# Low parts of projection weights made by an accumulating DMA instead of a VectorE subtraction

## The chip, the cores and the metric

The kernel runs on one core of a Trainium2 chip. The time is the device time of one execution, in microseconds; the kernel before has a median of 1444.12 us over three runs (1443.51 to 1444.13).

A core has five engines, each with its own queue of instructions, worked off in order: TensorE (PE) for matmuls, VectorE (DVE) and ScalarE (ACT) for elementwise work, GpSimd (POOL), and SyncE (SP), whose queue issues the DMAs. They wait for each other by semaphores. In this kernel a DMA is issued by SP, and after the change also by GpSimd.

## The reference

One layer on 1024 tokens of width 1024, all in float32. A mixer has two branches that start from one projection of `x`: forgetting attention with 8 heads of 64, and a gated linear recurrence (HGRN) with 4 heads of 128. Each branch is projected back to 1024 columns, weighted with a sigmoid gate, the two are added and projected once more. After a residual and a layer norm follows a SwiGLU network with 2816 hidden columns, another residual and another layer norm.

```
proj = x @ w_in
q_a, k_a, v_a, f_a, q_b, f_b, i_b, g_b, gate_a, gate_b = jnp.split(proj, IN_SPLITS, axis=-1)
...
merged = jax.nn.sigmoid(gate_a) * (y_a @ w_pa) + jax.nn.sigmoid(gate_b) * (y_b @ w_pb)
mix = merged @ w_o
```

## The kernel before

Every large product is made with operands split in two. The high part is the number rounded to the matmul's reduced format (`float32r`), the low part is what is left, and a product is three matmuls that add up in PSUM: high by high, high by low, low by high (`mm3`, line 449). The high part comes from ScalarE and the low part from VectorE (`split`, line 420):

```
def split(hi, lo, src):
    act.copy(hi, src)
    dve.tensor_sub(lo, src, f(hi))
```

Many of the products also go through a Strassen-Winograd scheme, which saves matmuls and costs VectorE additions. The change does not touch those. It touches the weights that are used plainly, through `weights` (line 437). Such a weight block of 128 rows by 1024 columns is loaded by SP into a raw tile (`wr0` or `wr1`, one buffer each) and split in two halves of 128 x 512, each with its own high tile and low tile (`wh0`, `wl0`, `wh1`, `wl1`, two buffers each). `weights` is called for:

- the q and k projections of head pairs 1 to 3 (`wq`, `wk`: 6 blocks), between the attention of one pair and the next;
- the three projections of each of the four HGRN heads (`wb`: 12 blocks);
- four gate blocks (`wg`) and four half gate blocks (`we`), which run beside attention and HGRN;
- the branch projections (`wp`: 8 blocks).

That is 34 blocks and 68 splits. The matmuls of a block stand in `project` (line 460), except those of `we`, which are in `gate_part` (line 1047). `project` runs over the eight chunks of 128 rows (four for `wp`) and makes the three matmuls of each chunk, for each half of 512 tokens.

The order of the work is not that of the source. Every call is recorded by `Plan`, which knows a cost for each operation (`cost`, line 131), a latency between engines (`LAT`, `OWN`) and the buffers, and places the calls one after another where they can start earliest (`schedule`, line 170). It does so for up to 20 rounds with ranks that come from the latest possible starts of the round before (`latest`, line 294), keeps the order with the earliest planned end, and writes each engine's calls in that order (`issue`, line 352). `early` lets the calls of a weight rank before their place in the source. The order of each engine is fixed when the program is built; on the chip a late operand makes the engine wait.

## Time and profile before

| | |
|---|---|
| median of three runs | 1444.12 us |
| span of the profiled execution, first to last instruction | 1441.5 us (its whole time is not given apart) |
| granted TensorE clock | 0.998 |
| PE busy | 1430.0 us, 99% |
| DVE busy | 1112.8 us, 77% |
| ACT busy | 668.6 us, 46% |
| POOL busy | 87.2 us, 6% |
| DMA on SP's queue | 180.11 MB, 37.9% of the 16 engines' span |

All instructions of the main part have line 363 in the profile, because they are issued from one helper. They are told apart by their tiles: `wb_h` and `wb_l` are high and low parts of an HGRN weight, `bps` the PSUM tile of its product, `gps`, `ge` and `pps` those of `wg`, `we` and `wp`, `gs` the gates made by the Strassen scheme, `fa`, `fb`, `fc` and `p` the products of the SwiGLU network.

### The profile page before, as it was taken

Reading aid. Unit: us, or ns where it says so; the run is one execution under the profiler, and the core shown is the slowest. Engines: PE = TensorE matmul, PEld = TensorE weight load, DVE = VectorE, ACT = ScalarE, POOL = GpSimd, SP = SyncE. Lnnn points to the kernel's source line nnn. Section 1 sums busy time; section 2 is a strip of 40 time slices with the busy share of each in tenths; the row PEclk is TensorE's granted clock in tenths of the full one; section 3 lists DMA queues with packets and bytes.
Section 4 is the critical chain, followed back from the end, with each engine's and each line's share of the span. In section 5 each row is a group of like instructions: output and inputs, shape, how many; then the busy total and the mean of one; then the engine's idle time right before and its main releaser. Section 6 shows DMA issues by size and latency. Waiting matters only on the chain.

```text
span 1441.5 us, 18901 instructions
## 1 busy us (share of the span) xinstructions
PE 1430.0 (99%) x6782; PEld 1188.2 (82%) x6782; DVE 1112.8 (77%) x1952; ACT 668.6 (46%) x1167; POOL 87.2 (6%) x100
## 2 busy tenths in 40 slices
PE   9999999999999999999999999999999999999997
PEld 7788888888888888788888888888888888888886
DVE  8998778567998999845857997666677776798596
ACT  5547768667767663344511443323333334434330
POOL 0002213120100110000000000000000000000011
PEclk9999999999999999999999999999999999999999
DMA  7022212211111455858500233233333326977632
GB/s 270 32 89 67 95 60 74 63 60 51 38 59 46 153 170 164 255 181 290 176 0 2 102 95 124 96 110 110 110 110 110 97 92 201 346 276 235 209 129 85
DMA packets 74029, 181.30 MB, mean 126 GB/s; under 512 B 8384, under 2 KB 9792, under 8 KB 73936
## 3 DMA queue, kind: packets, MB, share of 16 engines
q1 hardware_dynamic: 73936, 180.11, 37.9%
q8 instruction: 53, 0.87, 0.3%
q14 instruction: 40, 0.33, 0.1%
HBM read 139.90 MB, written 40.17 MB: 125 GB/s over the span
## 4 chain that ended last, share of the span: by engine, by line
PE 97%; DVE 2%; DMA 1%; issue 0%; ACT 0%; SPq 0%; DVEq 0%; ACTq 0%
PE p L363 14%; PE fb L363 12%; PE bps L363 9%; PE fc L363 8%; PE fa L363 8%; PE o L363 6%; PE pps L363 6%; PE gs L363 5%; PE vx L363 4%; PE gps L363 3%; PE s L363 2%; PE pv L363 2%; PE qps L363 2%; PE kps L363 2%; PE vy L363 2%; PE pt L363 2%
## 5 line engine op out<-in xcount | busy, mean ns | idle before, releaser
L363 PE MATMUL p<-dp 128*128 128x512 f32 (+1 forms) x957 | 210.1, 382 | 0.0
L363 PEld LDWEIGHTS p<-dp 128*128 128x128 f32 x957 | 175.1, 188 | 34.8
L363 PE MATMUL fc<-xs,Tp 128*128 128x512 f32 x528 | 127.3, 389 | 0.6 <-ACT Tp L363 0.6
L363 PE MATMUL fb<-xs,Tp 128*128 128x512 f32 x528 | 127.2, 389 | 0.0
L363 PEld LDWEIGHTS fc<-xs,Tp 128*128 128x128 f32 x528 | 99.1, 188 | 21.6 <-ACT Tp L363 1.0
L363 PEld LDWEIGHTS fb<-xs,Tp 128*128 128x128 f32 x528 | 99.1, 188 | 20.5
L363 PE MATMUL fa<-x,Tp 128*128 128x512 f32 x480 | 115.6, 389 | 0.0
L363 ACT CAST Tp<-t 128x512 fp32r<-128x512 f32 x88 | 54.2, 619 | 118.8 <-PE fc L363 64.8
L363 DVE TENSOR_TENSOR Tp<-t,Tp 128x512 fp32r<-128x512 f32 x88 | 60.6, 690 | 60.5 <-ACT Tp L363 59.9
L363 PEld LDWEIGHTS fa<-x,Tp 128*128 128x128 f32 x480 | 90.1, 188 | 18.7
L363 PE MATMUL bps<-xh,wb_h 128*128 128x512 f32 x192 | 76.2, 397 | 0.0
L363 PE MATMUL bps<-xl,wb_h 128*128 128x512 f32 x192 | 76.0, 396 | 0.0
L363 PE MATMUL bps<-xh,wb_l 128*128 128x512 f32 x192 | 75.5, 396 | 0.0
L363 POOL TENSOR_TENSOR norm<-norm,mhalf 128x1 f32<-128x1 f32 x16 | 17.2, 1075 | 886.3 <-DVE norm L363 886.3
L363 ACT CAST dp<-dap 128x1024 fp32r<-128x1024 f32 (+1 forms) x42 | 41.0, 979 | 57.8 <-PE p L363 35.7
L363 POOL TENSOR_SCALAR p<-p,soft 128x384 f32<-128x384 f32 (+4 forms) x64 | 51.9, 817 | 261.0 <-DVE soft L363 235.2
L363 DVE TENSOR_TENSOR tl<-pt,th 128x512 fp32r<-128x512 f32 (+1 forms) x96 | 52.2, 554 | 19.7 <-ACT th L363 15.5
L363 ACT CAST th<-pt 128x512 fp32r<-128x512 f32 (+1 forms) x96 | 45.5, 479 | 34.9 <-PE pt L363 30.8
L363 DVE TENSOR_TENSOR dp<-dap,dp 128x1024 fp32r<-128x1024 f32 (+1 forms) x42 | 47.4, 1132 | 15.9 <-ACT dp L363 15.7
L363 PE MATMUL fb<-x,Tp 128*128 128x512 f32 x240 | 57.7, 389 | 0.0
L363 PE MATMUL pt<-ident,p 128*128 128x128 f32 x288 | 53.8, 273 | 0.0
L363 ACT CAST Tp<-wg_r 128x512 fp32r<-128x512 f32 x40 | 24.9, 623 | 62.1 <-PE fb L363 30.2
(565 smaller groups left out, 3476.6 us busy)
## 6 DMA issues: line engine op xcount, KB each, us to landing
dbp<-in_w_fo SPq DMA_DIRECT2D x45, 512.0 KB, 5.3
dap<-a_d SPq DMA_DIRECT2D x35, 512.0 KB, 4.3
wg_r<-in_w_ff SPq DMA_DIRECT2D x22, 512.0 KB, 4.0
wu_r<-in_w_ff SPq DMA_DIRECT2D x22, 512.0 KB, 3.6
a_d<-ar SPq DMA_DIRECT2D x42, 256.0 KB, 2.7
a_d<-as SPq DMA_DIRECT2D x33, 256.0 KB, 3.4
wg_r<-in_w_g SPq DMA_DIRECT2D x16, 512.0 KB, 4.4
sg<-gate_d SPq DMA_DIRECT2D x32, 256.0 KB, 3.4
```

What stands on the lines that cost most here:

```text
L363: getattr(q.engine, method)(*args, **kw)
```

## The change

The high part stays a copy by ScalarE. The low part is no longer a subtraction on VectorE. ScalarE writes the negated high part into the low tile, and GpSimd issues a DMA that adds the same 128 x 512 part of the raw weight from HBM onto it. In `project`, all matmuls with the high part of the weight come first and those with the low part last, so that a block's low part is first read 16 matmuls after its high part (8 for `wp`). `gate_part` keeps its order.

The planner learns of the new DMA: it costs GpSimd's queue 1000 ns, its data counts as landed 2300 ns plus bytes/200 ns later, and a fourth one waits until the first of three has landed. The space for descriptors of GpSimd's DMAs grows from 256 to 512. Since the planner weighs all calls together, the order changes on all engines, in stages with no such weight too.

```diff
+RING = 3
...
+    SOFT, LANDS = 1000.0, 2300.0
...
-        if method == "copy_predicated":
+        if method == "copy_predicated" or "accum_op" in kw:
             ins.append(outs[0])
...
+        self.lands.append(self.LANDS + o_bytes(outs[0]) / 200.0 if q.name == "POOL" and method == "dma_start" else 0.0)
...
         if eng == "POOL":
+            if method == "dma_start":
+                return self.SOFT
...
+        ring = [0.0] * RING
...
+                    if self.lands[i]:
+                        t = max(t, ring[-RING])
...
-                fin = t + d
-                free[q] = fin
+                free[q] = t + d
+                fin = t + d + self.lands[i]
+                if self.lands[i]:
+                    ring.append(fin)
...
-        lat = self.OWN[q] if uq == q else self.LAT[q]
+        lat = self.lands[i] + (self.OWN[q] if uq == q else self.LAT[q])
...
-            split(hi, lo, raw[:, i * n:(i + 1) * n])
+            part = slice(i * n, (i + 1) * n)
+            act.copy(hi, raw[:, part])
+            act.activation(lo, f(hi), AF.Copy, scale=-1.0)
+            pool.dma_start(lo, src[:, part], accum_op=ALU.add)
...
         for c in range(kcs):
             rh, rl = (src or X)(c)
-            mm3(o, *w[c], rh[:, hs(hf)], rl[:, hs(hf)], c == 0, c == kcs - 1)
+            mm(o, w[c][0], rh[:, hs(hf)], start=c == 0, stop=False)
+            mm(o, w[c][0], rl[:, hs(hf)], start=False, stop=False)
+        for c in range(kcs):
+            mm(o, w[c][1], (src or X)(c)[0][:, hs(hf)], start=False, stop=c == kcs - 1)
...
-    nc = bacc.Bacc("TRN2", target_bir_lowering=False, num_devices=1, dynamic_dma_scratch_size=256)
+    nc = bacc.Bacc("TRN2", target_bir_lowering=False, num_devices=1, dynamic_dma_scratch_size=512)
```

More of the change, by code (lines that the diff above doesn't have):

```diff
@@ L54, in __getattr__, with o_bytes @@
         return lambda *args, **kw: self.plan.add(self, method, args, kw)
+def o_bytes(ap):
+    return ap.partition_size() * ap.free_size() * 4
 class Plan:
@@ L69, in __init__ @@
         self.early = 0
+        self.lands = []
         self.loose = set()
@@ L303, in latest @@
             for m in by.get(old, ()):
-                users[m].append((i, self.LAT[calls[m][0].name] + 60))
+                users[m].append((i, self.lands[m] + self.LAT[calls[m][0].name] + 60))
         preds = [[] for _ in calls]
```

## The prediction

> **What bounds the kernel now.** I read the engine totals first, then TensorE's own waits, then stretches of the span, and last the chain.

> ```profile
> span 1441.5 us, 18901 instructions
> PE 1430.0 (99%) x6782; PEld 1188.2 (82%) x6782; DVE 1112.8 (77%) x1952; ACT 668.6 (46%) x1167; POOL 87.2 (6%) x100
> ```

> TensorE (PE) is busy for all but 11.5 us. Every other engine has room as a mean, but a mean says little, so the waits come next (engine, line, what was waited for: total us, times, longest).

> ```profile
> PE vy L363 <- DVE mhalf L363: 1.2, 1, 1.2
> PE gs L363 <- DVE gu L363: 1.2, 2, 0.8
> PE fc L363 <- ACT Tp L363: 0.6, 1, 0.6
> ```

> Those three are all the waits the trace finds for PE: 3.0 us, one of them at the very start. None is in a stage that uses `weights` and `project`. The next view has busy time by stretch: attention with the q/k projections and plain gates, the recurrence (HGRN) with its projections, the half gates, and the branch projections.

> ```profile
> core 0: us, PE busy (x) PEld busy (x) DVE busy (x) ACT busy (x) POOL busy (x), PEclk, DMA share, GB/s
> 100.00:324.00 224.00, 223.98 (x1205) 188.31 (x1204) 165.28 (x497) 159.36 (x340) 51.88 (x64) 1.00 0.24 77
> 324.00:480.00 156.00, 156.00 (x839) 133.89 (x838) 133.53 (x218) 109.87 (x185) 10.32 (x12) 1.00 0.18 55
> 480.00:520.00 40.00, 40.00 (x228) 34.67 (x228) 36.98 (x55) 26.28 (x53) 3.54 (x2) 1.00 0.57 190
> 600.00:710.00 110.00, 109.64 (x484) 90.55 (x483) 70.33 (x106) 51.78 (x80) 0.00 (x0) 1.00 0.65 219
> ```

> PE is full in all four although VectorE reaches 86% (133.53 of 156) and 92% (36.98 of 40). A full PE can still hide short delays, since a matmul is on record for 0.39 us and the next starts earlier.

> ```profile
> 327.76 21.84 PE bps L363 x96
> 308.83 0.38 PE L363 MATMUL pt<-ident,p 128*128 128x128 f32 x2
> 308.97 0.31 PE L363 MATMUL pv<-tl,vhl 128*128 128x128 f32 x1
> 309.16 0.49 PE L363 MATMUL bps<-xh,wb_h 128*128 128x512 f32 x1
> 309.49 0.39 PE L363 MATMUL bps<-xl,wb_h 128*128 128x512 f32 x1
> 309.72 0.39 PE L363 MATMUL bps<-xh,wb_l 128*128 128x512 f32 x1
> ```

> From the chain, 96 projection matmuls take 21.84 us, 0.2275 each; a 128-wide one takes 0.07 (two from 308.83 to 308.97). From 309.16 to 309.49 is 0.33, so about 0.1 us of delay can hide between two matmuls. The change leaves number and widths of the matmuls as they are. So the floor stays, and only delays can be won or lost.

> **The change, part by part.**

> *VectorE.* 68 subtractions for low parts go.

> ```profile
> L363 DVE TENSOR_TENSOR wb_l<-wb_r,wb_h 128x512 fp32r<-128x512 f32 x24 | 16.4, 685 | 4.0 <-PE bps L363 2.4 <-ACT wb_h L363 1.5
> L363 DVE TENSOR_TENSOR wp_l<-wp_r,wp_h 128x512 fp32r<-128x512 f32 x16 | 10.9, 682 | 2.4 <-ACT wp_h L363 2.4
> L363 DVE TENSOR_TENSOR wg_l<-wg_r,wg_h 128x512 fp32r<-128x512 f32 x8 | 5.5, 690 | 0.0
> L363 DVE TENSOR_TENSOR we_l<-we_r,we_h 128x512 fp32r<-128x512 f32 x8 | 5.5, 682 | 0.2 <-issue 0.2
> L363 DVE TENSOR_TENSOR wk_l<-wk_r,wk_h 128x512 fp32r<-128x512 f32 x6 | 4.7, 778 | 6.7 <-ACT wk_h L363 6.6
> L363 DVE TENSOR_TENSOR wq_l<-wq_r,wq_h 128x512 fp32r<-128x512 f32 x6 | 4.1, 688 | 0.7 <-ACT wq_h L363 0.6
> ```

> 16.4 + 10.9 + 5.5 + 5.5 + 4.7 + 4.1 = 47.1 us of VectorE, all beside a full PE: worth nothing on the path by itself. The one VectorE wait in mid-kernel (gs, 1.2 us) lies at 585 and 604 us, before the first wp_l, so nothing is removed in front of it.

> *ScalarE.* 68 negated copies of 512 columns come. The nearest rows, with the high-part copy that precedes each:

> ```profile
> L363 ACT CAST wb_h<-wb_r 128x512 fp32r<-128x512 f32 x24 | 14.8, 621 | 21.1 <-PE bps L363 19.1 <-issue 1.7 <-PE kps L363 0.4
> 405.11 2.38 ACT L363 ACTIVATE box<-box 128x512 f32<-128x512 f32 x4 [2.23 <-DVE box L363]
> ```

> Four in a row take 2.38, so 0.6 each (0.62 for one on record): 68 x 0.6 = 41 us. In the recurrence it is some 24 of them, 14 us, on 109.87 of 156: 80%, hidden under PE. If ScalarE were the cover lost, a whole copy late (0.62) in each of the 14 close blocks below would be 8.7 us. The first row shows more: 19.1 of its 21.1 us of idle end on PE. The high buffers come free only when PE has used the weight before, so every step behind that copy is counted from PE.

> *GpSimd and the DMA.* 68 accumulating DMAs of 256 KB come, each waiting on GpSimd's queue for its negated copy. Behind a waiting one stand the softmax scalings and the powers of the norms; GpSimd is busy 51.88 of 224 us in attention and 10.32 of 156 after it, and no row has PE waiting for it, so I take zero; a scaling 1 us late for each of the 10 q, k and gate weights that are made in attention would cost up to 10. What matters is the time from issue to landing, call it L. The trace has no DMA from GpSimd and none that accumulates. Nearest rows (KB each, median us from issue to landing; the last three are instructions of GpSimd):

> ```profile
> wb_r<-in_w_b SPq DMA_DIRECT2D x12, 512.0 KB, 3.7
> xg_r<-in_xT SPq DMA_DIRECT2D x8, 512.0 KB, 5.3
> sg<-gate_d SPq DMA_DIRECT2D x32, 256.0 KB, 3.4
> dap<-a_d SPq DMA_DIRECT2D x7, 256.0 KB, 2.6
> L363 POOL TENSOR_SCALAR p<-p,soft 128x128 f32<-128x128 f32 x8 | 4.3, 539 | 195.9 <-DVE soft L363 194.4 <-PE pv L363 1.6
> L363 POOL TENSOR_SCALAR p<-p,soft 128x1024 f32<-128x1024 f32 x8 | 9.1, 1132 | 4.7 <-DVE soft L363 4.6
> L363 POOL TENSOR_TENSOR ss<-ss,mhalf 128x4 f32<-128x4 f32 x8 | 13.0, 1623 | 91.6 <-DVE ss L363 91.6
> ```

> A plain load of this size takes 2.6 to 3.4. Reading the destination as well can cost nothing, or as much as 256 KB more: 3.7 - 2.6 = 1.1. GpSimd's own part of the issue lies between nothing and its longest instruction, 1.6; I take 1.0, the middle of its rows (0.5 to 1.6). Traffic beside it adds more: the raw load of the next weight goes out earlier. Before, it waited for the subtraction:

> ```profile
> SPq L363 <- DVE wb_l L363: 58.9, 8, 11.6
> q1 hardware_dynamic: 73936, 180.11, 37.9%
> ```

> Now the raw tile is free after the high copy, and in the changed order that 512 KB load stands 0.7 to 1.1 us ahead of the first accumulation of most close blocks. So L runs from 2.6 to 3.4 + 1.1 + 1.6 = 6.1 in quiet stretches. I take 3.4 + 1.1 + 1.0 = 5.5: the 3.4 because its stretch has neighbours in the queue, as here. By the queue row, 256 KB occupy all 16 engines for 0.379 x 1441.5 / 180.11 x 0.262 = 0.8 us, so 16 accumulations of wp at once or twice that put 13 to 25 us on 0.65 x 110 = 71 us of 110: not full, and their first use is 7 us or more away, mostly 16. I price those at zero; if the gate loads slipped 0.3 us for each of 16, it would be 5.

> [...]

> *Low products last.* What covers L is PE work between the DMA's place in the order and the first matmul that reads the low part. The planner writes all calls in order of planned start, so I count the matmuls between the two in the changed program, 0.227 for a 512-wide one, less in proportion for narrower ones, 0.08 for a 128-wide. Of 68 DMAs, 29 have over 14 us, 14 have 7.1 to 9.5, and 25, in 14 blocks, have under 6.6. Shorter lead of each such block: wk1 5.9, wk2 5.3, wk3 5.5, wb0_0 5.2, wb2_0 6.5, wb1_1 5.8, wb0_1 5.6, wb2_1 5.2, wb1_2 5.4, wb0_2 5.5, wb2_2 5.9, wb1_3 4.9, we8 5.3, we12 5.6. PE runs its queue in order, so each block stalls for L minus its lead. Summed over blocks: 0.3 us at L = 5.2, 1.7 at 5.5, 4.5 at 5.8, 8.2 at 6.1, 12.1 at 6.4, 20.3 at 7.0.

> For the twelve wk and wb blocks I take 5.5: 1.5 us. we8 and we12 lie in the stretch with DMA share 0.57, among the xg loads, where 512 KB takes 5.3 instead of 3.7; 1.6 more gives 7.1, and stalls of 1.8 + 1.5 = 3.3.

> *PE's queue.* The changed program has 11 fewer separate wait instructions on PE (136 for 147). At the 0.1 us seen above that is -1.1; the other end is nothing.

> *Sum.* 1441.5 + 1.5 + 3.3 - 1.1 = 1445.2 for the span. The median of the runs, 1444.12, stands 2.6 above the profiled span, which has no separate whole time; the same 2.6 gives 1447.8, +0.25%. About 0.2%, 2.9 us, is what a measurement of this kernel can tell from no change.

> **The rivals.**

> *The accumulation is hidden anyway.* L stays at or below 5.2 everywhere. For it: the 2.6 us row plus 1.1 plus 1.0 is 4.7, under every lead in the list. Against it: the raw load and the xg loads in the same moments. Stalls 0.3, less 1.1: 1443.3.

> *The accumulation is much slower.* [...] 12.1 to 20.3, plus 1.5 for the crowded blocks, less 1.1: 1457 to 1465.
> [...]

> *Faster.* Relief of VectorE lets the gs products at 585 and 604 and the fc product run without their 1.2 and 0.6 us: with -1.1 and no stall, 1441.2. It decides when VectorE reaches gu some 0.8 us earlier. Against it: no wp_l stands ahead of that place, and 0.8 us is the most that one of these waits held.

> *The gate loads slip* in 600 to 710: the 5 us above, 1448 to 1453 with the other stalls.

> **How the numbers follow.** Forecast with stalls of 2 to 8 us net 0.41; hidden anyway 0.27; much slower 0.20; faster 0.07; gate loads 0.05. The predicted time is the forecast's. Its own range is 1445 to 1452. The range to hold 8 in 10 goes from 1442 (hidden, with the small wins) to 1464 (L near 7). Faster by 0.2% needs under 1441.2: 0.07. Within 0.2% (to 1447.0): 0.27 and a quarter of the forecast, 0.38. Slower: 0.55.

> **What would show it.** PE waits put down to DMA landings of wb_l, wk_l, we_l, near 0.1 to 2 us each, longest at we8 and we12; the accumulations at 5 to 6 us from issue to landing; VectorE at about 1066 us, ScalarE at about 710; raw loads starting sooner. Wrong: landings under 5 us and no new PE wait, or landings over 6.4 and one wait in each of 13 blocks, or waits of PE on GpSimd's scalings.

## The result, and the profile after

The changed kernel takes 1488.24 us, median of its runs (1486.20 to 1495.14), against 1444.12 before: a ratio of 1.031, interval 1.030 to 1.033. It is 44 us slower. The forecast was 1447.8 with a range up to 1464, so the direction was right and the size was wrong by a factor of 12.

The totals of the changed kernel (busy us, share of the span, instructions), to be laid beside those of before:

```profile
span 1484.4 us, 19006 instructions
PE 1447.2 (97%) x6782; PEld 1194.9 (80%) x6782; DVE 1074.7 (72%) x1884; ACT 701.1 (47%) x1233; POOL 143.5 (10%) x168
```

The span grew by 42.9 us. The number of matmuls is the same, yet PE is busy 17.2 us longer, and the other 25.7 us are new idle time of PE. The list of waits of the changed kernel (engine, line, what was waited for: total us, times, longest) names what PE idles on; before, no landing was in it:

```profile
PE bps L378 <- DMA wb_l<-in_w_b: 7.7, 6, 2.5
PE pps L378 <- DMA wp_l<-in_w_p: 5.6, 3, 2.4
PE kps L378 <- DMA wk_l<-in_w_qk: 4.1, 2, 2.2
PE ge L378 <- DMA we_l<-in_w_g: 3.7, 1, 3.7
PE gs L378 <- ACT Tgp_12h L378: 1.6, 1, 1.6
PE qps L378 <- DMA wq_l<-in_w_qk: 1.3, 1, 1.3
PE pt L378 <- POOL p L378: 1.2, 1, 1.2
```

That is 22.4 us in 13 waits for accumulating DMAs, for every kind of weight but wg. The busy time that was added has another face. In the view by stretches (us; PE, PEld, DVE, ACT and POOL busy with their counts; granted clock; DMA share; GB/s), the first three rows are a stretch with the wait for wp_l that ends at 664.49, and the two stretches behind it. The last three are the same around the wait of 2.51 us for wb_l that ends at 479.00:

```profile
661.97:665.38 3.41, 1.06 (x5) 0.76 (x5) 0.00 (x0) 0.45 (x1) 0.62 (x1) 1.00 0.98 293
665.38:668.80 3.42, 3.42 (x10) 2.65 (x9) 1.38 (x2) 1.22 (x2) 0.26 (x1) 0.50 0.77 180
668.80:672.21 3.41, 3.41 (x17) 2.83 (x16) 0.69 (x1) 2.92 (x5) 0.88 (x1) 1.00 0.79 203
...
474.23:477.65 3.42, 2.26 (x14) 1.66 (x13) 2.96 (x5) 2.66 (x4) 0.87 (x1) 1.00 0.29 50
477.65:481.06 3.41, 2.06 (x13) 1.88 (x14) 0.39 (x1) 0.60 (x1) 0.00 (x0) 1.00 0.15 27
481.06:484.47 3.41, 3.41 (x25) 3.06 (x24) 3.34 (x6) 3.04 (x4) 0.00 (x0) 1.00 0.00 0
```

Behind the wait for wp_l PE counts as full, but the granted clock is 0.50 for 3.4 us, and 10 matmuls pass where 17 pass in the next 3.4 us. The same happens behind the waits that end at 224.63, 288.80, 532.91 and 718.91, and at 617.60, where PE waited 1.62 and 1.13 us for operands of the gates and not for a low part. That makes six places. Half of PE's busy time at the low clock is lost: 1.7 us at four of them, 1.5 at 617.60 and 3.1 behind the wait for we_l, together 11.4 of the 17.2 us. The other 5.8 us stand at the full clock. A matmul is on record for 0.39 us and the next starts 0.23 behind it, so up to 0.16 us at each wait, and delays shorter than that, count as busy time (an estimate from these two numbers). Behind the last three rows the clock does not fall (1.00); the end of this document sets this place beside the six. At those six a wait of TensorE is paid twice.

Why do the weights come late? For most of them, not because one accumulation takes long. The DMA view (KB each, median us from issue to landing):

```profile
q0 software_dynamic: 9792, 17.83, 7.6%
...
sg<-gate_d SPq DMA_DIRECT2D x32, 256.0 KB, 4.8
wb_l<-in_w_b POOLq DMA_DIRECT2D x24, 256.0 KB, 4.2
wp_l<-in_w_p POOLq DMA_DIRECT2D x16, 256.0 KB, 5.3
```

4.2 us is under the 5.5 that the forecast took, and with 4.2 no wait was to come. (Three of the waits end on landings that were long by themselves, in stretches crowded with loads: the we_l DMA behind the longest wait is issued at 524.76 and lands 8.1 us later, and the two wp_l DMAs behind the waits that end at 664.49 and 718.91 take 7.5 and 7.9; the DMA share is 0.98, 0.91 and 1.05 while they are out.) The timeline around the first q weight shows what is wrong (start, us, engine, line, instruction, idle time before it and its releaser):

```profile
105.51 0.63 ACT L378 ACTIVATE wq_l<-wq_h 128x512 fp32r<-128x512 f32 x1
106.46 1.03 POOL L378 DMA_DIRECT2D wq_l<-in_w_qk  x1 [106.03 <-PE vy L378]
106.68 0.63 ACT L378 ACTIVATE wq_l<-wq_h 128x512 fp32r<-128x512 f32 x1
112.53 0.90 POOL L378 DMA_DIRECT2D wq_l<-in_w_qk  x1 [5.04 <-ACT p L378]
```

The second negated copy ends at 107.31, and the DMA that adds to it starts at 112.53, 5.2 us later. The first lands after 5.8 us, the longest of the wq_l landings, at 112.27: 0.26 us ahead of the second's start. The program holds no wait of the one for the other. So it goes throughout: of the 68 DMAs, none starts before the one ahead of it has landed; the shortest distance from landing to start is 0.26 us, and where the next one's negated copy was ready it is 0.26 to 0.32. The list of GpSimd's waits has many of that kind, put down to "issue", that is to nothing that the profile shows:

```profile
POOL wp_l L378 <- issue: 20.1, 3, 7.3
POOL wb_l L378 <- issue: 16.5, 4, 5.1
POOL we_l L378 <- issue: 9.8, 2, 7.5
POOL wk_l L378 <- issue: 7.8, 2, 3.9
```

The theory formed from this: the space for descriptors of GpSimd's DMAs holds only one accumulating DMA of 128 x 512, not the three of the planner's RING. The second of a pair then starts when the first has landed, and its low part comes mostly 6 to 10 us after its negated copy (9.1 for the second wq_l). The rivals: the accumulation itself is slow or crowded; low products last is a worse order by itself; the new order on ScalarE and GpSimd costs time whatever the DMA does.

### The profile page after: what moved, and what is told of

The parts are those of the page before. It is cut to its first block, busy times and chain, and to the rows that moved or that the text cites. A ratio compares the mean times of both kernels' runs of the same rounds, so it can differ in the third digit from the quotient of the medians.

```text
span 1484.4 us, 19006 instructions
## 1 busy us (share of the span) xinstructions
PE 1447.2 (97%) x6782; PEld 1194.9 (80%) x6782; DVE 1074.7 (72%) x1884; ACT 701.1 (47%) x1233; POOL 143.5 (10%) x168
## 3 DMA queue, kind: packets, MB, share of 16 engines
q1 hardware_dynamic: 73936, 180.11, 36.6%
q0 software_dynamic: 9792, 17.83, 7.6%
## 4 chain that ended last, share of the span: by engine, by line
PE 79%; issue 11%; DMA 4%; DVE 2%; POOL 2%; ACT 2%; SPq 0%; DVEq 0%; POOLq 0%; ACTq 0%
PE p L378 14%; PE fb L378 11%; PE fc L378 8%; PE fa L378 8%; PE o L378 6%; PE gs L378 4%; PE vx L378 4%; PE gps L378 3%; PE vy L378 2%; PE bps L378 2%; PE pps L378 2%; PE s L378 2%; PE pv L378 2%; PE qps L378 2%; PE pt L378 2%
## 5 line engine op out<-in xcount | busy, mean ns | idle before, releaser
L378 PE MATMUL bps<-xh,wb_l 128*128 128x512 f32 x192 | 53.9, 402 | 7.7 <-DMA wb_l<-in_w_b 7.7
L378 POOL TENSOR_SCALAR p<-p,soft 128x640 f32<-128x640 f32 (+5 forms) x64 | 53.4, 864 | 57.1 <-DVE soft L378 52.0
## 6 DMA issues: line engine op xcount, KB each, us to landing
dbp<-in_w_fo SPq DMA_DIRECT2D x45, 512.0 KB, 5.3
dap<-a_d SPq DMA_DIRECT2D x35, 512.0 KB, 4.4
wg_r<-in_w_ff SPq DMA_DIRECT2D x22, 512.0 KB, 3.8
wu_r<-in_w_ff SPq DMA_DIRECT2D x22, 512.0 KB, 3.6
a_d<-ar SPq DMA_DIRECT2D x42, 256.0 KB, 2.6
a_d<-as SPq DMA_DIRECT2D x33, 256.0 KB, 3.3
wg_r<-in_w_g SPq DMA_DIRECT2D x16, 512.0 KB, 4.8
sg<-gate_d SPq DMA_DIRECT2D x32, 256.0 KB, 4.8
```

Of the source, the lines that this page charges most:

```text
L378: getattr(q.engine, method)(*args, **kw)
```

## The experiments

Times are medians, each with the ratio to the kernel before, measured beside it on the same chip.

| run | us | ratio, interval |
|---|---|---|
| changed kernel | 1488.2 | 1.031 (1.030 to 1.033) |
| low products last alone | 1446.3 | 1.002 (1.001 to 1.003) |
| ... and negated copy, added by VectorE | 1444.6 | 1.000 (0.999 to 1.001) |
| changed order, plain copies for the additions | 1447.2 | 1.002 (1.001 to 1.003) |
| changed kernel, low products in place | 1478.1 | 1.024 (1.022 to 1.026) |
| RING 1 | 1461.4 | 1.011 (1.009 to 1.014) |
| RING 1, wp by VectorE | 1452.5 | 1.006 (1.003 to 1.008) |
| RING 1, later landing | 1465.0 | 1.014 (1.012 to 1.016) |
| RING 1, later landing, wp by VectorE | 1460.4 | 1.011 (1.010 to 1.013) |
| small mask table, space 512 | 1508.6 | 1.044 (1.043 to 1.046) |
| small mask table, space 1024 | 1465.0 | 1.015 (1.013 to 1.018) |
| ... wp by VectorE | 1461.2 | 1.012 (1.010 to 1.014) |
| ... plain copies | 1453.7 | 1.007 (1.005 to 1.009) |
| ... later landing | 1452.7 | 1.005 (1.004 to 1.007) |

### The parts that do not accumulate

The first run has only the order of the matmuls, on the kernel before; the second adds the negated copy on ScalarE and lets VectorE do the addition.

```diff
-            mm3(o, *w[c], rh[:, hs(hf)], rl[:, hs(hf)], c == 0, c == kcs - 1)
+            mm(o, w[c][0], rh[:, hs(hf)], start=c == 0, stop=False)
+            mm(o, w[c][0], rl[:, hs(hf)], start=False, stop=False)
+        for c in range(kcs):
+            mm(o, w[c][1], (src or X)(c)[0][:, hs(hf)], start=False, stop=c == kcs - 1)
```

> The kernel before, with only the order of the matmuls in project changed: high-part products first, low-part products last; low parts by VectorE subtraction as before. Theory A and B: no effect of its own, 1442 to 1447. Rival C (the order of the matmuls or the new arrangement of all calls costs the time): above 1455.

```diff
-            split(hi, lo, raw[:, i * n:(i + 1) * n])
+            part = slice(i * n, (i + 1) * n)
+            act.copy(hi, raw[:, part])
+            act.activation(lo, f(hi), AF.Copy, scale=-1.0)
+            dve.tensor_add(lo, f(lo), raw[:, part])
```

> Low products last, and the low part made from the negated copy on ScalarE plus an addition of the raw tile on VectorE, no DMA from GpSimd. It holds the 68 added ScalarE copies and keeps 68 VectorE operations. Theory A and B: 1442 to 1449, ScalarE near 710 us busy. Rival D (the load on ScalarE costs the time): above 1455.

They ran at 1446.3 and 1444.55, both as the theory had it. The order costs at most 4 us, and 68 copies more on ScalarE cost nothing that can be measured. The third keeps the changed kernel's order on every engine and replaces each addition by a copy of the raw weight:

```diff
-            pool.dma_start(lo, src[:, part], accum_op=ALU.add)
+            pool.dma_start(lo, src[:, part])
```

> The changed kernel in the very same order on every engine, but GpSimd's DMA only copies the raw part over the low tile and adds nothing, so the low part is wrong and is left out of the result's meaning. If one at a time belongs to the adding, the second DMA of a pair starts about 1 us after the first and the time falls to 1455 to 1470. If it belongs to GpSimd's DMA queue with this space for descriptors, the starts still follow the landings and the time stays at 1475 to 1490, a little lower as a copy lands up to 1.1 us sooner.

1447.2 us, lower than either window: 41 of the 44 us go when the DMA copies instead of adding. Here each DMA starts where it stands in the order, as the prediction had it, though it lands sooner than the prediction's 5.5. Its GpSimd timeline at the place shown above:

```profile
106.21 0.71 POOL L378 DMA_DIRECT2D wq_l<-in_w_qk  x1 [105.78 <-PE vy L378]
107.37 0.54 POOL L378 DMA_DIRECT2D wq_l<-in_w_qk  x1 [0.45 <-ACT wq_l L378]
```

its DMA view:

```profile
q0 software_dynamic: 9792, 17.83, 4.4%
...
wb_l<-in_w_b POOLq DMA_DIRECT2D x24, 256.0 KB, 3.5
wp_l<-in_w_p POOLq DMA_DIRECT2D x16, 256.0 KB, 5.3
```

and its list of PE's waits, with the one landing that is in it:

```profile
PE gs L378 <- DVE gu L378: 1.3, 1, 1.3
...
PE ge L378 <- DMA we_l<-in_w_g: 0.2, 1, 0.2
```

Two copies are in flight at once: the second starts 1.16 us behind the first, as soon as its negated copy is done, and the six of wq_l take a median of 4.0 us to land. So the order on ScalarE, GpSimd and SP is not the cause; adding is. It does two things: the second of a pair waits, and the same bytes occupy the 16 DMA engines longer (0.076 x 1484.4 / 17.83 x 0.262 = 1.66 us per 256 KB against 0.044 x 1444.1 / 17.83 x 0.262 = 0.93).

### How many are in flight

Three small kernels do nothing of the layer: SP copies x to the output, and GpSimd issues six accumulating and six plain DMAs of 128 x 512. They differ in the space for descriptors: 512, 1024 and 4096. Each was run once.

```diff
-SCRATCH = 512
+SCRATCH = 1024
```

> Not the layer: x is copied to the output, and beside that GpSimd issues six accumulating and six plain DMAs of 128 x 512 into twelve tiles with no dependence among them, descriptor space 512. Both theories on the cause (space for descriptors, or the adding itself): plain ones start about 0.6 us apart, accumulating ones only after the landing of the one before, 4 us apart.

> The same DMAs with descriptor space 1024. If the space is the cause, with an accumulating DMA taking about twice the descriptors of a plain one, at least two accumulating DMAs are now in flight and start about 0.9 us apart. If the adding itself is done one at a time: still 4 us apart.

> The same with descriptor space 4096. Space: all six accumulating DMAs start 0.9 us apart. The adding itself: still 4 us apart.

GpSimd's timeline with a space of 512:

```profile
1.24 1.74 POOL L37 DMA_DIRECT2D pla<-in_x  x3 [0.79 <-PEq L51]
7.93 0.54 POOL L37 DMA_DIRECT2D pla<-in_x  x1 [4.96 <-issue]
...
31.19 0.88 POOL L35 DMA_DIRECT2D acc<-in_x  x1 [3.97 <-issue]
35.12 0.88 POOL L35 DMA_DIRECT2D acc<-in_x  x1 [3.06 <-issue]
39.16 0.88 POOL L35 DMA_DIRECT2D acc<-in_x  x1 [3.16 <-issue]
```

Three plain DMAs start one behind the other, and the fourth 0.3 us after the first has landed (7.62). Accumulating ones go singly, each 0.3 us after the landing of the one before (30.88, 34.81, 38.85). With a space of 1024:

```profile
3.45 0.96 POOL L35 DMA_DIRECT2D acc<-in_x  x1
7.49 0.89 POOL L35 DMA_DIRECT2D acc<-in_x  x1 [3.07 <-issue]
11.45 0.87 POOL L35 DMA_DIRECT2D acc<-in_x  x1 [3.07 <-issue]
16.02 0.86 POOL L35 DMA_DIRECT2D acc<-in_x  x1 [3.71 <-issue]
```

Here the first three start before any of them has landed (15.71), and the fourth 0.3 us behind that. They start 4 us apart and not 0.9, as was expected: four plain DMAs were issued ahead of them, and the second starts 0.3 us after the first landing of those (7.23); GpSimd is idle for 3.07 us ahead of the third as well. With 4096 four start one behind the other within 3.62 us, not all six; the fifth comes at 7.64, and what it waits for was not shown. The whole run is no shorter than with 1024, 39.8 us for both. So the theory's first half is shown: with 512, RING = 3 is right for plain copies and wrong for additions. The kernels of the whole layer agree: in the changed kernel, with 512, no adding DMA is ever out beside another one. In the run with 1024 and the later landing, below, three start at 354.79, 355.83 and 356.43, where no landing of wb_l, the first of them, takes less than 3.6 us.

### More room in the kernel

To make room in the kernel for a space of 1024, the table of masks is made smaller. It is held four times over; held twice, with the masked copy of its user made in two halves, it is loaded with 94.5 KB instead of 156.5, and 496 bytes per partition come free. The first of the pair has only that, as the partner; the second has the space as well, and the same order on every engine.

```diff
-MASKS = 1 + 4 * 62 + 64
+MASKS = 1 + 2 * 62 + 64
...
-dynamic_dma_scratch_size=512
+dynamic_dma_scratch_size=1024
```

> The changed kernel with a smaller mask table (tiled twice instead of four times, so each predicated copy of the recurrence's middle levels is done in two halves, 20 more on VectorE); 496 bytes per partition come free. Descriptor space stays 512, so that this is the partner of the next run. Theory (an accumulating DMA needs more than half of the space of 512, so only one is in flight): like the changed kernel, 1478 to 1495.

> The very same order on every engine as the run before, descriptor space 1024. Theory: three accumulating DMAs fit, as the planner counts on, second DMAs of a pair start about 1 us after the first, PE's waits on wk_l and wb_l go, and the time falls by 25 to 40 us, to 1446 to 1460; what is left are wp_l and we_l, where SP's loads share the engines. Rival (traffic alone): within 8 us of the run before.

1508.6 and 1465.0, both above their windows: the partner is 20 us slower than the changed kernel, whose space and RING it has, so the small table and the order planned with it cost time of their own while one DMA is in flight. But the space alone, with all instructions in the same order, is worth 43.6 us. GpSimd's waits for "issue" in the partner,

```profile
POOL wp_l L378 <- issue: 46.4, 8, 8.9
POOL wb_l L378 <- issue: 15.0, 3, 8.0
```

have gone with the room of 1024:

```profile
POOL wb_l L378 <- issue: 0.7, 3, 0.3
```

and so have most of PE's: the partner's 19.9 us for wb_l in nine waits become 4.3 in four. That settles the greater part. 21 us over the kernel before remained, and three more runs on this base looked for their cause. The first takes wp back to VectorE, the second copies instead of adding (so the addition is left out), the third gives the planner a landing time 3.7 us longer.

```diff
-            act.copy(hi, raw[:, part])
-            act.activation(lo, f(hi), AF.Copy, scale=-1.0)
-            pool.dma_start(lo, src[:, part], accum_op=ALU.add)
+            if name[:2] == "wp":
+                split(hi, lo, raw[:, part])
+            else:
+                ...
```

> Space 1024, and wp's low parts by VectorE's subtraction; 52 accumulating DMAs are left. If wp among SP's loads is the rest: 1443 to 1448, that is no slower than the kernel before by more than 0.3%. If not: like the run before it, above 1450.

> The order, the small mask table and the descriptor space of 1024 of the earlier run, but GpSimd's DMAs copy the raw weight instead of adding it, so the low part is wrong and the addition is left out. If the 20 us that stay with a space of 1024 come from the longer landings of the adding DMAs, this runs at 1445 to 1449 us with no wait of TensorE over 1.5 us. If they come from the order that the planner wrote or from the two mask operations, it stays at 1460 or more.

```diff
-    SOFT, LANDS = 1000.0, 2300.0
+    SOFT, LANDS = 1000.0, 6000.5
```

> Small mask table, descriptor space 1024, adding DMAs, and the planner's landing time raised by 3.7 us (6000.5 for 2300.0, plus 1.3 us by size, 7.3 us in all), near what the trace shows for a pair that lands together. If the 20 us that stay are landings that the planner does not know, it gains most of them: 1445 to 1452 us, waits of TensorE on wb_l under 2 us in sum. If they are traffic beside SP's loads or the clock, which no order cures, it stays above 1456.

The first gave 1461.2, so wp is only some 4 us of the 21. The second came out between its two cases, at 1453.7: of the 21 us, 11 go with the addition, and 10 stay in an order that has no accumulation at all. Of PE's waits there, 3.6 us are still on landings of GpSimd's plain copies (2.1 on we_l, 1.5 on wb_l), and 3.4 on gu, VectorE's sums for the gates made by the Strassen scheme. The third gave 1452.7, just outside the window that was set, and has no wait of PE on a low part's landing any more, although wb_l lands after 4.9 us, later than in the changed kernel. The first rows of PE's waits there, and what the longest of them goes back to on ScalarE:

```profile
PE pps L378 <- DVE sg L378: 3.9, 1, 3.9
PE gs L378 <- DVE gu L378: 1.3, 2, 0.9
...
690.52 0.63 ACT L378 ACTIVATE sg<-sg 128x512 f32<-128x512 f32 x1 [9.83 <-DMA sg<-gate_d]
```

So an order that knows how long an addition takes, with room for more than one, keeps the low parts from stopping PE. It does not do so for free. The wait of 3.9 us is for sg, the gates that weight the branch projections. It goes back to a gate load by SP for which ScalarE stands idle 9.83 us, and the clock falls behind it (0.72 granted from 690 to 695 us, 0.94 in the next five), another 1.7: 5.6 of the 9 us that are left. The DMA share is 1.05 to 1.06 from 665 to 690, and the wp_l additions take a median of 6.7 us; that they hold the gate load up was not shown. The small table was not run without GpSimd's DMAs, so what it costs by itself stays open, and with it the rest in both runs, whose orders differ.

### An order for one in flight

The other way is to leave the space and tell the planner the truth. RING 3 becomes 1; then wp goes back to VectorE; then both again with a landing time 2.2 us longer.

```diff
-RING = 3
+RING = 1
```

> The changed kernel, with one number altered: the planner lets only one accumulating DMA be in flight instead of three, and orders the work for that. Theory A (in the changed kernel each such DMA starts only when the one before it has landed, e.g. landed at 112.27 and next started at 112.53, while the order allowed for three at once): most of the ten waits of PE on wk_l, wb_l and we_l go, about 16 us idle and much of the slow clock behind them; 1455 to 1468 us, with the waits on wp_l left. Theory B (each DMA by itself lands late, because of traffic or the adding): the waits stay, 1480 to 1492.

> One in flight in the planner, and the low parts of the branch projection weights (wp) made by VectorE's subtraction again; the other 52 still by accumulating DMA. In the run with one in flight, PE's waits on wp_l were 6.7 us, with 726.1 - 623.9 = 102 us from the first to the last pps product against 92.7 before. If the accumulating DMAs in that stretch, where SP's loads fill the queues, are what is left: 1446 to 1452, gate loads back from 4.7 to about 3.4 us, clock 0.998. If the rest is elsewhere: above 1456.

1461.4 and 1452.5, the second half a microsecond above its window. RING alone gets 27 of the 44 us back, and wp costs 8 to 9 of what stays (7.8 by the two ratios). PE's waits with RING 1:

```profile
PE pps L378 <- DMA wp_l<-in_w_p: 6.7, 4, 2.8
PE ge L378 <- DMA we_l<-in_w_g: 2.0, 2, 1.0
PE bps L378 <- DMA wb_l<-in_w_b: 0.8, 1, 0.8
```

wb_l fell from 7.7 to 0.8 and wk_l left the list; the wp weights, sixteen that go singly in about 100 us, were not helped by this order.

```diff
-    SOFT, LANDS = 1000.0, 2300.0
+    SOFT, LANDS = 1000.0, 4500.0
```

> Full mask table and descriptor space 512. The planner counts one adding DMA in flight and a landing 2.2 us later than in the changed kernel (4500 for 2300, plus 1.3 by size, 5.8 in all), near the landings that the traces show beside SP's loads. If what RING = 1 leaves (17 us) is landing time that the planner does not know, this gains most of the waits on wb_l, wk_l and we_l (2.8 us in that run's list, with the clock after them): 1452 to 1457 us, with wp_l as it was. If wp is the whole rest, it stays at 1459 to 1463.

> As the run with RING = 1 and wp made by VectorE (1452.5), with the landing time 2.2 us later. If landings are what stays there, 1444 to 1448 us and no wait of TensorE on a landing over 0.5 us. If it is the order that the planner writes for the other stages, 1450 to 1455 as before.

Both missed on the slow side: 1465.0 and 1460.4, the second with a wait of 2.2 us left on we_l. In the first no landing of a low part is left among PE's longer waits; others took their place:

```profile
PE pps L378 <- DVE sg L378: 3.9, 1, 3.9
PE kdt L378 <- DVE kd L378: 2.2, 2, 2.0
PE gs L378 <- DVE at L378: 1.2, 1, 1.2
...
PE pps L378 <- ACT wp_h L378: 1.1, 1, 1.1
```

The wait for sg points to the same source as above: loads of sg by SP stand with 1% of the span in the chain that ended last. The mean granted clock of that run is 0.995, against 0.998 before. It may be that the planner, with one DMA in flight and 5.8 us each, makes room for the weights by putting other work late. These runs don't show that, nor where the rest of the 21 us is.

### Low products in place

> The changed kernel with the old order of matmuls in project (low product of each chunk right after its high ones), space 512, planner with three in flight. The cover of 16 matmuls (3.6 us) for the low part is gone, and the planner knows it, so it must make the weights earlier or put other work in between. Theory: slower than the changed kernel or equal, 1485 to 1530; if the low products last were themselves at fault, it would be faster, below 1475.

```diff
-            mm(o, w[c][0], rh[:, hs(hf)], start=c == 0, stop=False)
-            mm(o, w[c][0], rl[:, hs(hf)], start=False, stop=False)
-        for c in range(kcs):
-            mm(o, w[c][1], (src or X)(c)[0][:, hs(hf)], start=False, stop=c == kcs - 1)
+            mm3(o, *w[c], rh[:, hs(hf)], rl[:, hs(hf)], c == 0, c == kcs - 1)
```

1478.1 us, 10 faster than the changed kernel, where slower was expected: wb_l holds PE for 4.3 us in two waits instead of 7.7 in six. A reading that fits, and was not tested: sixteen matmuls between the parts look to the planner like room for a DMA, and it uses that room up to a landing time that is false; without them it makes the weights earlier.

No version runs faster than the kernel before. The nearest, with VectorE doing the addition, has an interval that holds 1.

## Why the prediction was right or wrong

*Right: the bound, and what it made free.* PE sets the time, and relief of VectorE is worth nothing: it is 38.1 us less busy (1112.8 to 1074.7) and nothing was gained. The ScalarE copies are hidden (1444.55 with them). Low products last, priced at nothing by itself, measured 1.002, at most 4 us. The waits stand where they were to stand: on wb_l, wk_l and we_l, the longest in the half gates, at 3.7. There the size came near too, 3.3 us forecast in two waits, but with luck: the landing took 8.1 where 7.1 was reckoned, and its DMA had first stood 5.1 us behind the one before it.

*Wrong: the step "PE runs its queue in order, so each block stalls for L minus its lead".* The lead was counted from the DMA's place in the order. It was taken for granted that the DMA starts there once its negated copy is ready. Every block has two DMAs close together, and the second starts only when the first has landed. Where the two stand closest, as in most wb and wk blocks, its time from ready to landing is about 4 us of waiting plus 4.2 of its own, over every one of the 14 leads, which lie between 4.9 and 6.5. The term "L" itself was not low: 4.2 to 4.3 for wb and wk, below the 4.7 at which the first rival would have seen no stall. With plain copies, which do start where they stand, the time was 1447.2 and the forecast 1447.8, but that is luck: the stalls that the forecast summed, 4.8 us, were 0.2 there, and the rest is other small delays.

*What would have shown it.* The working weighed how long a DMA takes and not how many may be out. The diff raises the space for descriptors and puts RING beside it; that the two go together is a claim of the change, and no row of the kernel before could bear it out, since it has no DMA from GpSimd. It should have been a rival by itself: "one in flight", each second DMA later by one landing. With the forecast's own 5.5 us that makes 11 us to the second landing of a pair, and most blocks late by 4 to 5 us.

*Missing: the clock.* A stall was priced at its length. 11.4 of the 42.9 us are matmuls made slow at a granted clock of 0.50, most of them behind a stall. The place that shows it best is the half gate's, where PE waited 3.71 us:

```profile
532.91 0.79 PE L378 MATMUL ge<-xh,we_l 128*128 128x512 f32 x1 [3.71 <-DMA we_l<-in_w_g]
533.50 0.63 PE L378 MATMUL ge<-xh,we_h 128*128 128x512 f32 x1
```

A matmul that is on record for 0.39 elsewhere takes 0.63 there. The end of this document has the other places, where the clock fell after shorter waits.

*Mis-sized: wp at zero.* "First use is 7 us or more away" counted each of the 16 as started at its place. They go singly, in a stretch whose DMA share is 0.83, and use up their leads: 5.6 us of waits and two stretches of slow clock. With RING 1, the kernel without them is 8.9 us faster (1461.4 to 1452.5). The gate loads did slip, sg from 3.4 to 4.8, the rival of 0.05, but sg left no wait on PE's list in the changed kernel. In three later runs it left one of 3.9 to 4.2.

*Mis-sized: zero for the queue behind a waiting DMA.* One scaling of the softmax held PE, 1.2 us; up to 10 had been named as the other end.

*The "-1.1" for 11 fewer waits of PE* can't be told among these sizes. The 2.6 us that the sum added from span to time were 1.8 in the changed kernel (1486.20 for a span of 1484.4). *The rival "much slower"* had the sign and the place, stalls in close blocks, but by a slower transfer; its 1457 to 1465 stopped where L was 7, and here the second of a close pair lands mostly 7 to 10 us after it could have started (the second wq_l: ready to be added to at 107.31, released to PE at about 116.4). One transfer by itself was not that slow: in the small kernel with a space of 512 an addition with nothing beside it lands after 3.7 us (35.12 to 38.85) and a plain copy after 3.0 (43.08 to 46.07), both below the 5.5 that was taken for L.

## What to carry to other kernels

When work moves to a queue of DMAs, ask how many may be in flight before asking how long one takes, and measure that with a kernel of six DMAs; here the second of a pair told it, starting 0.3 us after the landing of the first. A planner's constant for such a limit is part of the change and has to be true for the form that is used, here an adding DMA and not a plain one: with the true one 27 of the 44 us came back, and with the wrong one an order that hides everything on paper hid less than the old order did. And price a wait of a full TensorE at its length plus the slow clock that can follow, here 1.5 to 1.7 us at a place where the clock fell, and 3.1 at one.
